# Attention on halves of TensorE's array: scores on 64 rows each, outputs side by side on 64 columns each

## The chip, the core and the metric

The kernel runs on one core of one Trainium2 chip. Its time is the device time of one execution in microseconds (us). Most executions of one kernel agree within 0.3%. TensorE (PE in the profile) multiplies and writes to PSUM, VectorE (DVE) and ScalarE (ACT) read PSUM and compute, GpSimd (POOL) does elementwise work and some DMAs, and SyncE (SP) issues most DMAs. Weight loads of TensorE stand apart as PEld.

## The reference, cut to what matters

Two large blocks follow each other; the change is in the first one's attention. There are 512 tokens, 16 query heads of width 64 in 2 groups of 8, and each group shares one key and one value head:

```
def one_block(args):                       # i: one of 4 blocks of 128 queries
    kb = dynamic_slice(kp, start, 2 * BLOCK); vb = dynamic_slice(vp, start, 2 * BLOCK)
    sc = einsum('bqhgd,bkhd->bhgqk', qi, kb) * ATTN_SCALE
    sc = where(mask, sc, NEG_INF)          # causal, window of 128
    sc = concatenate([sc, sink], axis=-1)
    p = softmax(sc, axis=-1)[..., :-1]
    return einsum('bhgqk,bkhd->bqhgd', p, vb)
```

## The kernel before

Activations lie with features on the 128 partitions and the 512 tokens along the free axis. `kv[:, 0]` holds the keys of both groups: group 0 on partitions 0 to 63, group 1 on partitions 64 to 127. `kv[:, 1]` holds the values. The queries in `q` are permuted so that each of its 8 tiles of 128 partitions holds one head of group 0 (partitions 0 to 63) above one head of group 1 (64 to 127).

`attention` walks through 16 cases: 4 blocks `b` of 128 queries times 4 pairs `hg` of query tiles. `weights(b, hg)` makes the scores of four heads (L325, tile `q` stationary, keys moving), masks them (L328), and takes the softmax on DVE and ACT (L338 to L350). A block sees 256 keys, the first one 128. Before the change a score matmul contracts over all 128 partitions, against `kz`, a copy of the keys in which the other group's 64 partitions are zero; GpSimd makes `kz` (L244, L245) early in the block. `apply(b, hg)`, called one case later, transposes the weights by TensorE (L363), copies them out of PSUM (L365, tile `pT`), and multiplies by the transposed values `vt` (L367): group `r` writes 64 PSUM partitions of `po`, so its matmul uses 64 columns of the array, and both its key blocks run one after the other before the next group's transposes begin. `split` (L84, L85) then writes the result as a high and a low part into `ya`.

These matmuls are f32; each shows in the trace as two MATMUL rows with a weight load each. The other matmuls of this stretch, `mm3` at L111 (gates on `xb`, the pooling's projection on `yp`), are f32r with 512 columns and show as one. They are the work that fills the attention: after each case `block1` issues one more unit out of the list `fill` (three gates, then `mix`, then gates and `pool_up` in turn). A list scheduler of the framework sets the order of the instructions on each engine ahead of time; on the chip each engine takes its instructions in that order and waits on semaphores. `mix` is the pooling branch: DVE and ACT make `pf` (L399 to L401, L84, L85), which the matmuls at L408 read.

Elsewhere in the kernel, matmuls on parts of the array already stand side by side. In the RWKV chunks (second block) L1252 gives two heads 64 columns each, and L1147 and L1159 give two heads 64 rows and 64 columns each:

```
for hh in range(2):                                        # L1252: heads are (hh, z, zb)
    nc.tensor.matmul(py[zb], vt[:, zb], sk[:, hh, 0, 1], start=True, stop=True)
for hh in range(2):                                        # L1147: rows z, columns zb
    nc.tensor.matmul(py[zb], s0[z], C[c][2][z, d], start=True, stop=True)
for hh in range(2):                                        # L1159: rows z, columns z
    nc.tensor.matmul(pq[z], C[c][0][z, d], s0[z], start=True, stop=True)
```

Here `z` is one half of the partitions and `zb` the other. L1104 uses 64 rows and all 128 columns, one head at a time.

Of the kernel before, what the change touches and what calls it, by code (L numbers as in the profile page):

```python
# [8 lines left out]
F32 = mybir.dt.float32  # L9
# [11 lines left out]
P = 128  # L21
T = 512
# [27 lines left out]
class Kern:  # L50
# [154 lines left out]
    def block1(self):  # L205

        nc, tc = self.nc, self.tc
        st = ExitStack()
        p1 = self.c1 = st.enter_context(tc.tile_pool(name="b1", bufs=1))
        wk = st.enter_context(tc.tile_pool(name="b1w", bufs=2))  # L210
# [10 lines left out]
        nc.scalar.copy(rs, self.rstd_row(self.rstd_cols(ss, 1e-5)))  # L221
        self.consts1()
        kv = p1.tile([P, 2, T], F32, name="kv")
        kz = p1.tile([P, 2, T], F32, name="kz")
        q = self.res.tile([P, KD, T], F32, name="q", tag="h")
        pz = p1.tile([P, 4, T], F32, name="pz")
        ya = self.Apool.tile([P, 2, KD, T], F32R, name="ya", tag="A")
        yah, yal = ya[:, 0], ya[:, 1]

        def zout(dst, m):  # L230
            f = AF.Identity if m < 14 else AF.Sigmoid

            def out(_, ps):
                t = self.t()
                nc.vector.tensor_tensor(t, ps, rs, op=OP.mult)
                nc.scalar.activation(dst, t, f, bias=self.v("b_in", m))
            return out

        X = self.rhs(xh, xl)
        for m in range(10):  # L240
            self.dense("w_in", X, zout(kv[:, m] if m < 2 else q[:, m - 2], m), [m])
        for r in range(2):
            z, zz = slice(r * 64, r * 64 + 64), slice(64 - r * 64, 128 - r * 64)
            nc.gpsimd.memset(kz[zz, r], 0.0)  # L244
            nc.gpsimd.tensor_copy(kz[z, r], kv[z, 0])  # L245
        for m in range(10, 14):
            self.dense("w_in", X, zout(pz[:, m - 10], m), [m])
        pf = p1.tile([P, 2, 4, T], F32R, name="pf", tag="t2")
# [21 lines left out]
            fill += [lambda m=m + GA1: gate(m)] * (m < 8 - GA1) + [lambda m=m: pool_up(m)]  # L270
        fill += [lambda m=m: gate_a(m) for m in range(8)]
        steps, done, n = 0, 0, len(fill)
        for _ in self.attention(wk, kv, kz, q, yah, yal):
            steps += 1
            while done < min(n, (steps - 1) * FA):
                fill[done]()
                done += 1
# [26 lines left out]
        st.close()  # L304
        return h, xg, ss

    def attention(self, wk, kv, kz, q, yah, yal):
        nc = self.nc
        vt = wk.tile([P, 4, P], F32, name="vt", bufs=1)
        ps = self.aux().rearrange("p (b c) -> p b c", b=4)  # L310
        for b in range(4):
            nc.tensor.transpose(ps[:, b], kv[:, 1, b * P:(b + 1) * P], self.ident)
        nc.scalar.copy(vt, ps)
        sink = self.sink
        cases = [(b, hg) for b in range(4) for hg in range(4)]
        S = {}

        def weights(b, hg):
            nk = P if b == 0 else 2 * P
            k0 = 0 if b == 0 else (b - 1) * P  # L320
            s = S[b, hg] = wk.tile([P, 2, 2, 2 * P], F32, name="sc", tag="sc", bufs=3)
            pr = [self.aux().rearrange("p (h k) -> p h k", h=2) for _ in range(2)]
            for i in range(2):
                for r in range(2):
                    nc.tensor.matmul(pr[r][:, i, :nk], q[:, hg * 2 + i, b * P:(b + 1) * P],  # L325
                                     kz[:, r, k0:k0 + nk], start=True, stop=True)
            for r in range(2):
                nc.vector.scalar_tensor_tensor(  # L328
                    s[:, r, :, :nk], pr[r][:, :, :nk], 0.125,
                    self.amask[:, None, 2 * P - nk:].to_broadcast([P, 2, nk]),  # L330
                    op0=OP.mult, op1=OP.add)
            mx = wk.tile([P, 2, 2], F32, name="mx", tag="mx")
            ng = wk.tile([P, 2, 2], F32, name="ng", tag="ng")
            sm = wk.tile([P, 2, 2], F32, name="sm", tag="sm")
            es = wk.tile([P, 2, 2], F32, name="es", tag="es")
            rc = wk.tile([P, 2, 2], F32, name="rc", tag="rc")
            sk = sink[:, :, hg * 2:hg * 2 + 2]
            nc.vector.tensor_reduce(mx, s[:, :, :, :nk], axis=AX.X, op=OP.max)  # L338
            nc.vector.tensor_tensor(mx, mx, sk, op=OP.max)
            nc.vector.tensor_scalar(ng, mx, -1.0, None, op0=OP.mult)  # L340
            nc.vector.tensor_tensor(es, sk, mx, op=OP.subtract)
            for r in range(2):
                for i in range(2):
                    nc.scalar.activation(s[:, r, i, :nk], s[:, r, i, :nk], AF.Exp, bias=ng[:, r, i:i + 1],
                                         accum_out=sm[:, r, i:i + 1])
            nc.scalar.activation(es, es, AF.Exp)
            nc.vector.tensor_tensor(sm, sm, es, op=OP.add)
            nc.vector.reciprocal(rc, sm)
            for r in range(2):
                nc.vector.tensor_tensor(s[:, r, :, :nk], s[:, r, :, :nk],  # L350
                                        rc[:, r, :, None].to_broadcast([P, 2, nk]), op=OP.mult)

        def apply(b, hg):
            nk = P if b == 0 else 2 * P
            k0 = 0 if b == 0 else (b - 1) * P
            s = S.pop((b, hg))
            po = self.aux()[:, :2 * P]
            nb = nk // P
            for r in range(2):
                pt = self.aux().rearrange("p (b h q) -> p b h q", b=2, h=2)  # L360
                for kb in range(nb):
                    for i in range(2):
                        nc.tensor.transpose(pt[:, kb, i], s[:, r, i, kb * P:(kb + 1) * P], self.ident)  # L363
                pT = wk.tile([P, 2, 2 * P], F32, name="pT", tag="pT", bufs=3)
                nc.scalar.copy(pT[:, :nb], pt[:, :nb].rearrange("p b h q -> p b (h q)"))  # L365
                for kb in range(nb):
                    nc.tensor.matmul(po[r * 64:r * 64 + 64], vt[:, k0 // P + kb, r * 64:r * 64 + 64], pT[:, kb],  # L367
                                     start=kb == 0, stop=kb == nb - 1)
            self.split(po.rearrange("p (h q) -> p h q", h=2),
                       yah[:, hg * 2:hg * 2 + 2, b * P:(b + 1) * P],  # L370
                       yal[:, hg * 2:hg * 2 + 2, b * P:(b + 1) * P])

        for i, c in enumerate(cases):
            weights(*c)
            if i:
                apply(*cases[i - 1])
            yield 1
        apply(*cases[-1])
        yield 1

# [1320 lines left out]
```

## Time and profile before

| | |
|---|---|
| three timed runs, median | 2801.33 us (2794.91 to 2803.78) |
| the profiled execution | 2801.58 us, of which the span of instructions is 2799.8 us |
| PE busy | 2661.8 us (95%) |
| DVE, ACT, POOL busy | 1929.1 us (69%), 1222.7 us (44%), 746.6 us (27%) |
| the attention, first score matmul to last output matmul | about 97 to 245 us of the span |

Busy time is a share of the whole span; what counts here is who waits for whom within the attention's 148 us. A matmul's own duration in the trace overlaps with the next one's, so the time that it takes from TensorE is read from the start of one row to the start of a later one.

### The profile page before, as it was taken

The numbers are of one execution on the slowest core, as the hardware profiler recorded it, in microseconds if no ns is written. First come the engines' busy times: TensorE is split into PE (matmuls) and PEld (weight loads), VectorE is DVE, ScalarE is ACT, GpSimd is POOL, SyncE is SP. The second block draws the span as 40 slices with busy tenths as digits, with TensorE's granted clock in tenths as the row PEclk, the third lists the DMA queues.
The fourth block names the chain that finished last, engine by engine and source line by source line (L and its number), as shares of the span: only waits on it lengthen the run. The fifth ranks groups of instructions, "written<-read, shape, count | busy, mean of one in ns | idle before, by whom it ended". The sixth has DMA issues, their size and how long they took to land.

```text
span 2799.8 us, 38104 instructions
## 1 busy us (share of the span) xinstructions
PE 2661.8 (95%) x13941; PEld 2202.5 (79%) x13941; DVE 1929.1 (69%) x3742; ACT 1222.7 (44%) x2124; POOL 746.6 (27%) x807
## 2 busy tenths in 40 slices
PE   8999999799999999999999998898899989999997
PEld 6777888789987788888888886676667778888886
DVE  4664579997666778887778858877687765545336
ACT  4664354566532333333333336445555545222234
POOL 0100110000022345454545511443544513111002
PEclk9999999899999999999999998999899999999999
DMA  3112322467798878898899952121000013222332
GB/s 122 61 42 76 118 101 84 141 200 241 245 346 288 300 267 324 327 330 314 321 331 332 323 176 91 61 61 46 1 1 1 1 46 107 91 98 91 98 98 76
DMA packets 173356, 446.15 MB, mean 159 GB/s; under 512 B 14192, under 2 KB 76784, under 8 KB 170992
## 3 DMA queue, kind: packets, MB, share of 16 engines
q1 hardware_dynamic: 136304, 309.47, 32.8%
q0 software_dynamic: 36864, 134.23, 13.3%
q8 instruction: 110, 1.80, 0.3%
q14 instruction: 78, 0.64, 0.1%
HBM read 404.33 MB, written 37.22 MB: 158 GB/s over the span
## 4 chain that ended last, share of the span: by engine, by line
PE 69%; DVE 14%; DMA 5%; POOL 4%; issue 4%; ACT 4%; SPq 0%; DVEq 0%; POOLq 0%; ACTq 0%
PE mm L111 46%; PE aux L782 10%; DMA ga<-gad 3%; PE mm L782 2%; DVE wlo L85 2%; PE aux L607 1%; PE mm L1285 1%; PE aux L367 1%; PE aux L325 1%; POOL gl_E L1379 1%; POOL gr L694 1%; PE aux L1212 1%; DVE gl_K L1388 1%; POOL t L915 1%; DMA wraw<-in_v_dram 1%
## 5 line engine op out<-in xcount | busy, mean ns | idle before, releaser
L84 ACT CAST whi<-wraw 128x1024 fp32r<-128x1024 f32 (+2 forms) x439 | 454.1, 1035 | 920.4 <-PE mm L111 764.2
L85 DVE TENSOR_TENSOR wlo<-wraw,whi 128x1024 fp32r<-128x1024 f32 (+2 forms) x439 | 569.1, 1297 | 319.6 <-ACT whi L84 295.9
L111 PE MATMUL mm<-xb,whi 128*128 128x384 f32 (+1 forms) x2656 | 732.8, 356 | 13.9 <-ACT whi L84 13.3
L111 PEld LDWEIGHTS mm<-xb,whi 128*128 128x128 f32 x2656 | 483.6, 190 | 59.2 <-ACT whi L84 28.5
L111 PE MATMUL mm<-xb,wlo 128*128 128x384 f32 (+1 forms) x1328 | 472.8, 356 | 11.7 <-DVE wlo L85 11.7
L694 POOL DMA_INDIRECT gr<-in_u_dram,gid x128 | 192.2, 1501 | 605.3 <-DVE ga L755 495.3
L111 PEld LDWEIGHTS mm<-xb,wlo 128*128 128x128 f32 x1328 | 252.2, 190 | 40.7 <-DVE wlo L85 21.8
L782 PE MATMUL aux<-wlo,wh 128*128 128x512 f32 x640 | 255.4, 399 | 12.3 <-DVE wlo L85 12.2
L694 POOL DMA_INDIRECT gr<-in_v_dram,gid x128 | 194.2, 1517 | 235.3 <-DVE ga L755 106.3
L782 PE MATMUL aux<-whi,wl 128*128 128x512 f32 x640 | 253.4, 396 | 0.0
L782 PE MATMUL aux<-whi,wh 128*128 128x512 f32 x640 | 253.2, 396 | 0.0
L111 PE MATMUL mm<-fx,whi 128*128 128x512 f32 (+1 forms) x736 | 223.2, 386 | 0.0
L111 PE MATMUL mm<-fp,whi 128*128 128x512 f32 (+1 forms) x732 | 200.6, 360 | 1.1 <-ACT fp L84 0.5
L711 DVE SCALAR_TENSOR_TENSOR yg<-gr,ag,yg 128x1024 f32<-128x1024 f32 x127 | 163.1, 1285 | 4.3 <-DMA gr<-in_v_dram,gid 1.8
L707 DVE SCALAR_TENSOR_TENSOR jk<-gr,xtd 128x1024 bf16<-128x1024 f32 x128 | 156.4, 1222 | 9.5 <-DMA gr<-in_u_dram,gid 7.1
L111 PEld LDWEIGHTS mm<-fx,whi 128*128 128x128 f32 x736 | 135.7, 188 | 30.8
L111 PE MATMUL mm<-x,whi 128*128 128x512 f32 x432 | 148.0, 424 | 8.4 <-DVE h L792 7.5
L782 PEld LDWEIGHTS aux<-wlo,wh 128*128 128x128 f32 x640 | 120.5, 188 | 43.1 <-DVE wlo L85 20.0
L111 PEld LDWEIGHTS mm<-fp,whi 128*128 128x128 f32 x732 | 129.6, 189 | 26.3 <-DVE fp L85 1.7
L111 PE MATMUL mm<-fx,wlo 128*128 128x512 f32 (+1 forms) x368 | 141.8, 385 | 0.0
L782 PEld LDWEIGHTS aux<-whi,wl 128*128 128x128 f32 x640 | 120.6, 188 | 24.6
L782 PEld LDWEIGHTS aux<-whi,wh 128*128 128x128 f32 x640 | 120.7, 189 | 24.4
(491 smaller groups left out, 4703.4 us busy)
## 6 DMA issues: line engine op xcount, KB each, us to landing
wraw<-in_uT_dram SPq DMA_DIRECT2D x128, 512.0 KB
wraw<-in_v_dram SPq DMA_DIRECT2D x128, 512.0 KB
wraw<-in_w_in_dram SPq DMA_DIRECT2D x57, 512.0 KB
Gd<-stg SPq DMA_DIRECT2D x24, 1024.0 KB
gt<-Gd SPq DMA_DIRECT2D x16, 1536.0 KB
wraw<-in_ffn_gate_dram SPq DMA_DIRECT2D x22, 512.0 KB
wraw<-in_ffn_up_dram SPq DMA_DIRECT2D x22, 512.0 KB
wraw<-in_ffn_down_dram SPq DMA_DIRECT2D x17, 512.0 KB
```

What stands on the lines that cost most here:

```text
L84: self.nc.scalar.copy(hi, src)
L85: return (eng or self.nc.vector).tensor_tensor(lo, src, unr(hi), op=OP.subtract)
L111: self.nc.tensor.matmul(ps, a, b, start=first and n == 1, stop=last and n == 3 * kt)
L325: nc.tensor.matmul(pr[r][:, i, :nk], q[:, hg * 2 + i, b * P:(b + 1) * P], kz[:, r, k0:k0 + nk], start=True, stop=True)
L367: nc.tensor.matmul(po[r * 64:r * 64 + 64], vt[:, k0 // P + kb, r * 64:r * 64 + 64], pT[:, kb], start=kb == 0, stop=kb == nb - 1)
L607: nc.tensor.matmul(ps[:, t], j1[:, z, t4 + t], oi[:, t4 + t], start=z == 0, stop=z == 1)
L694: dep(nc.gpsimd.indirect_dma_start(out=r, out_offset=None, in_=(A["u"], A["v"])[z], in_offset=bass.IndirectOffsetOnAxis(ap=gid[:, n:n + 1] ...
L707: i = nc.vector.scalar_tensor_tensor(jk, r, 1.0, xf, op0=OP.mult, op1=OP.mult, accum_out=ag[:, n:n + 1])
L711: i = nc.vector.scalar_tensor_tensor(yg, r, ag[:, n:n + 1], yg, op0=OP.mult, op1=OP.add)
L782: nc.tensor.matmul(acc[f][t], a[:, tk], b[:, fs].rearrange("p k g -> p (k g)"), start=n == 0 and j == 0, stop=n == P - 1 and j == 2)
L915: nc.gpsimd.tensor_tensor(s, z[:, :T], z[:, 2:], op=OP.add)
L1212: nc.tensor.matmul(ps, BK[:, 0, d], AR[:, :, d], start=True, stop=True)
```

## The change

The score matmuls read 64 partitions of `q` and of `kv[:, 0]` directly, group 0 on the array's rows 0 to 63 and group 1 on rows 64 to 127; groups alternate from one matmul to the next. `kz` with its two fills and two copies on GpSimd is gone. In `apply` the transposes and copies of both groups come first, and the output matmuls then alternate between the groups, that is between the two halves of the array's columns. `pT` gets a fourth buffer.

```
--- before.py
+++ after.py
@@ -221,7 +221,6 @@
         nc.scalar.copy(rs, self.rstd_row(self.rstd_cols(ss, 1e-5)))
         self.consts1()
         kv = p1.tile([P, 2, T], F32, name="kv")
-        kz = p1.tile([P, 2, T], F32, name="kz")
         q = self.res.tile([P, KD, T], F32, name="q", tag="h")
         pz = p1.tile([P, 4, T], F32, name="pz")
         ya = self.Apool.tile([P, 2, KD, T], F32R, name="ya", tag="A")
@@ -239,10 +238,6 @@
         X = self.rhs(xh, xl)
         for m in range(10):
             self.dense("w_in", X, zout(kv[:, m] if m < 2 else q[:, m - 2], m), [m])
-        for r in range(2):
-            z, zz = slice(r * 64, r * 64 + 64), slice(64 - r * 64, 128 - r * 64)
-            nc.gpsimd.memset(kz[zz, r], 0.0)
-            nc.gpsimd.tensor_copy(kz[z, r], kv[z, 0])
         for m in range(10, 14):
             self.dense("w_in", X, zout(pz[:, m - 10], m), [m])
         pf = p1.tile([P, 2, 4, T], F32R, name="pf", tag="t2")
@@ -270,7 +265,7 @@
             fill += [lambda m=m + GA1: gate(m)] * (m < 8 - GA1) + [lambda m=m: pool_up(m)]
         fill += [lambda m=m: gate_a(m) for m in range(8)]
         steps, done, n = 0, 0, len(fill)
-        for _ in self.attention(wk, kv, kz, q, yah, yal):
+        for _ in self.attention(wk, kv, q, yah, yal):
             steps += 1
             while done < min(n, (steps - 1) * FA):
                 fill[done]()
@@ -304,7 +299,7 @@
         st.close()
         return h, xg, ss
 
-    def attention(self, wk, kv, kz, q, yah, yal):
+    def attention(self, wk, kv, q, yah, yal):
         nc = self.nc
         vt = wk.tile([P, 4, P], F32, name="vt", bufs=1)
         ps = self.aux().rearrange("p (b c) -> p b c", b=4)
@@ -320,10 +315,12 @@
             k0 = 0 if b == 0 else (b - 1) * P
             s = S[b, hg] = wk.tile([P, 2, 2, 2 * P], F32, name="sc", tag="sc", bufs=3)
             pr = [self.aux().rearrange("p (h k) -> p h k", h=2) for _ in range(2)]
+
             for i in range(2):
                 for r in range(2):
-                    nc.tensor.matmul(pr[r][:, i, :nk], q[:, hg * 2 + i, b * P:(b + 1) * P],
-                                     kz[:, r, k0:k0 + nk], start=True, stop=True)
+                    z = slice(r * 64, r * 64 + 64)
+                    nc.tensor.matmul(pr[r][:, i, :nk], q[z, hg * 2 + i, b * P:(b + 1) * P],
+                                     kv[z, 0, k0:k0 + nk], start=True, stop=True)
             for r in range(2):
                 nc.vector.scalar_tensor_tensor(
                     s[:, r, :, :nk], pr[r][:, :, :nk], 0.125,
@@ -356,15 +353,19 @@
             s = S.pop((b, hg))
             po = self.aux()[:, :2 * P]
             nb = nk // P
+            pTs = []
             for r in range(2):
                 pt = self.aux().rearrange("p (b h q) -> p b h q", b=2, h=2)
                 for kb in range(nb):
                     for i in range(2):
                         nc.tensor.transpose(pt[:, kb, i], s[:, r, i, kb * P:(kb + 1) * P], self.ident)
-                pT = wk.tile([P, 2, 2 * P], F32, name="pT", tag="pT", bufs=3)
+                pT = wk.tile([P, 2, 2 * P], F32, name="pT", tag="pT", bufs=4)
                 nc.scalar.copy(pT[:, :nb], pt[:, :nb].rearrange("p b h q -> p b (h q)"))
-                for kb in range(nb):
-                    nc.tensor.matmul(po[r * 64:r * 64 + 64], vt[:, k0 // P + kb, r * 64:r * 64 + 64], pT[:, kb],
+                pTs.append(pT)
+
+            for kb in range(nb):
+                for r in range(2):
+                    nc.tensor.matmul(po[r * 64:r * 64 + 64], vt[:, k0 // P + kb, r * 64:r * 64 + 64], pTs[r][:, kb],
                                      start=kb == 0, stop=kb == nb - 1)
             self.split(po.rearrange("p (h q) -> p h q", h=2),
                        yah[:, hg * 2:hg * 2 + 2, b * P:(b + 1) * P],
```

The scheduler lays the first block's attention out anew on PE, DVE and ACT; GpSimd loses the four `kz` instructions, SP is as before, and the order behind the attention is as before on every engine. In the listings below one row is one matmul of the program (two rows of the trace where it is f32 and no transpose).

First place, PE just ahead of the pooling's first matmuls (L408, now L409), at 122.16 to 129.84 us of the trace. Before:

```order
L367 MATMUL aux<-pT,vt 64x256
L363 MATMUL aux<-ident,sc 128x128 x2
L325 MATMUL aux<-kz,q 128x256 x3
L367 MATMUL aux<-pT,vt 64x256
L325 MATMUL aux<-kz,q 128x256
L363 MATMUL aux<-ident,sc 128x128 x2
L367 MATMUL aux<-pT,vt 64x256
L363 MATMUL aux<-ident,sc 128x128 x2
L325 MATMUL aux<-kz,q 128x256 x2
L367 MATMUL aux<-pT,vt 64x256
L325 MATMUL aux<-kz,q 128x256 x2
L408 MATMUL mm<-pf,whi 128x512 x2
```

The same place now:

```order
L368 MATMUL aux<-pT,vt 64x256 x2
L322 MATMUL aux<-kv,q 128x256 x4
L361 MATMUL aux<-ident,sc 128x128 x4
L368 MATMUL aux<-pT,vt 64x256 x2
L322 MATMUL aux<-kv,q 128x256 x4
L409 MATMUL mm<-pf,whi 128x512 x2
```

The output matmuls, which stood alone in four places, stand in two pairs, and the score matmuls in two fours; two of the transposes have moved out of this place.

Second place, PE in the first case with 256 keys after `mix` (from about 148 us of the trace). Before:

```order
L325 MATMUL aux<-kz,q 128x256 x4
L363 MATMUL aux<-ident,sc 128x128 x4
L111 MATMUL mm<-yp,whi 128x512 x2
L111 MATMUL mm<-yp,wlo 128x512
L111 MATMUL mm<-yp,whi 128x512 x2
L111 MATMUL mm<-yp,wlo 128x512
L367 MATMUL aux<-pT,vt 64x256 x2
L363 MATMUL aux<-ident,sc 128x128 x4
```

The same place now:

```order
L322 MATMUL aux<-kv,q 128x256 x4
L361 MATMUL aux<-ident,sc 128x128 x8
L111 MATMUL mm<-yp,whi 128x512 x2
L111 MATMUL mm<-yp,wlo 128x512
L111 MATMUL mm<-yp,whi 128x512 x2
L111 MATMUL mm<-yp,wlo 128x512
L111 MATMUL mm<-yp,whi 128x512
L368 MATMUL aux<-pT,vt 64x256
L111 MATMUL mm<-yp,whi 128x512
L368 MATMUL aux<-pT,vt 64x256 x3
```

All eight transposes of a case come first, then its four output matmuls; here the scheduler has put one L111 between the first of the four and the other three.

## Rows read from the trace of the kernel before

**Rows 1.** The page: span, and the chain that ended last by line.

```profile
span 2799.8 us, 38104 instructions
...
PE mm L111 46%; PE aux L782 10%; DMA ga<-gad 3%; PE mm L782 2%; DVE wlo L85 2%; PE aux L607 1%; PE mm L1285 1%; PE aux L367 1%; PE aux L325 1%; POOL gl_E L1379 1%; POOL gr L694 1%; PE aux L1212 1%; DVE gl_K L1388 1%; POOL t L915 1%; DMA wraw<-in_v_dram 1%
```

**Rows 2.** Windows: length; PE, PEld, DVE, ACT, POOL busy (instructions); PEclk; DMA share, GB/s.

```profile
122.16:129.84 7.68, 7.16 (x31) 4.10 (x30) 7.36 (x20) 5.26 (x10) 0.00 (x0) 1.00 0.13 34
129.84:140.33 10.49, 7.73 (x22) 5.39 (x21) 10.14 (x21) 8.96 (x20) 0.00 (x0) 0.67 0.14 50
140.33:245.26 104.93, 104.93 (x481) 73.33 (x480) 67.51 (x146) 67.37 (x165) 0.00 (x0) 1.00 0.16 48
```

**Rows 3.** Waits, 97 to 247 us: who waited for whom; total, times, longest.

```profile
DVE t L235 <- PE mm L111: 11.8, 8, 3.5
...
DVE ya L85 <- ACT ya L84: 10.8, 8, 3.8
DVE sc L328 <- PE aux L325: 10.0, 9, 2.0
...
DVE t L258 <- PE mm L111: 7.2, 5, 3.1
DVE sm L347 <- ACT es L346: 6.9, 5, 2.4
...
PE mm L408 <- ACT pf L84: 2.5, 1, 2.5
```

**Rows 4.** Tile kz: instructions; ns min/median/max, first and last start in us, forms.

```profile
L325 PE MATMUL aux<-kz,q x128: 270/379/483, 97.4 to 230.2; 128*128 128x256 f32 x96, 128*128 128x128 f32 x32
...
L245 POOL COPY kz<-kv x2: 613/992/1370, 31.5 to 32.9; 64x512 f32<-64x512 f32 x2
```

**Rows 5.** Line L367, the output matmuls.

```profile
L367 PE MATMUL aux<-pT,vt x112: 379/379/431, 107.6 to 244.4; 128*64 128x256 f32 x112
```

**Rows 6.** Timeline of PE: start and length in us, line, rows*columns of the array, count.

```profile
153.61 0.40 PE L111 MATMUL mm<-yp,whi 128*128 128x512 f32 x1
153.94 1.08 PE L367 MATMUL aux<-pT,vt 128*64 128x256 f32 x4
154.95 0.50 PE L111 MATMUL mm<-yp,whi 128*128 128x512 f32 x1
155.28 0.39 PE L111 MATMUL mm<-yp,wlo 128*128 128x512 f32 x1
155.52 1.89 PE L325 MATMUL aux<-kz,q 128*128 128x256 f32 x8
157.06 0.82 PE L111 MATMUL mm<-xb,whi 128*128 128x512 f32 x2
157.71 0.39 PE L111 MATMUL mm<-xb,wlo 128*128 128x512 f32 x1
```

**Rows 7.** Timeline of PE in the second block: matmuls on parts of the array.

```profile
1977.49 0.44 PE L1252 MATMUL aux<-rc_sk,rc_vt 128*64 128x128 f32 x4 [0.25 <-POOL rc_sk L1249]
1977.86 0.69 PE L1095 MATMUL aux<-alo,lora 64*128 64x512 f32 x1
...
1983.34 1.12 PE L1104 MATMUL aux<-wlo,lora 64*128 64x512 f32 x2
1984.39 0.33 PE L1232 MATMUL aux<-ident,rkv 128*128 128x128 f32 x1
...
2083.39 0.33 PE L1147 MATMUL aux<-rc_RH,rw_S 64*64 64x128 f32 x2
2083.40 0.33 PE L1159 MATMUL aux<-rw_S,rc_PH 64*64 64x64 f32 x4
...
2092.07 0.65 PE L1147 MATMUL aux<-rc_RH,rw_S 64*64 64x128 f32 x8
2092.65 0.60 PE L1285 MATMUL mm<-rc_Ap,rc_SL 128*128 128x128 f32 x3
```

**Rows 8.** Window after the wait of L408: columns as in Rows 2.

```profile
133.80:138.00 4.20, 4.16 (x11) 3.01 (x12) 3.85 (x10) 3.49 (x7) 0.00 (x0) 0.50 0.36 125
```

More of the change, by code (lines that the diff above doesn't have):

```diff
@@ L223, in block1 @@
         kv = p1.tile([P, 2, T], F32, name="kv")
-        kz = p1.tile([P, 2, T], F32, name="kz")
         q = self.res.tile([P, KD, T], F32, name="q", tag="h")
@@ L241, in block1 @@
             self.dense("w_in", X, zout(kv[:, m] if m < 2 else q[:, m - 2], m), [m])
[L242 to L245, printed above, removed]
         for m in range(10, 14):
@@ L272, in block1 @@
         steps, done, n = 0, 0, len(fill)
-        for _ in self.attention(wk, kv, kz, q, yah, yal):
+        for _ in self.attention(wk, kv, q, yah, yal):
             steps += 1
@@ L305, in block1, with attention @@
         return h, xg, ss
-    def attention(self, wk, kv, kz, q, yah, yal):
+    def attention(self, wk, kv, q, yah, yal):
         nc = self.nc
@@ L324, in weights @@
                 for r in range(2):
-                    nc.tensor.matmul(pr[r][:, i, :nk], q[:, hg * 2 + i, b * P:(b + 1) * P],
-                                     kz[:, r, k0:k0 + nk], start=True, stop=True)
+                    z = slice(r * 64, r * 64 + 64)
+                    nc.tensor.matmul(pr[r][:, i, :nk], q[z, hg * 2 + i, b * P:(b + 1) * P],
+                                     kv[z, 0, k0:k0 + nk], start=True, stop=True)
             for r in range(2):
@@ L358, in apply @@
             nb = nk // P
+            pTs = []
             for r in range(2):
@@ L363, in apply @@
                         nc.tensor.transpose(pt[:, kb, i], s[:, r, i, kb * P:(kb + 1) * P], self.ident)
-                pT = wk.tile([P, 2, 2 * P], F32, name="pT", tag="pT", bufs=3)
+                pT = wk.tile([P, 2, 2 * P], F32, name="pT", tag="pT", bufs=4)
                 nc.scalar.copy(pT[:, :nb], pt[:, :nb].rearrange("p b h q -> p b (h q)"))
-                for kb in range(nb):
-                    nc.tensor.matmul(po[r * 64:r * 64 + 64], vt[:, k0 // P + kb, r * 64:r * 64 + 64], pT[:, kb],
+                pTs.append(pT)
+            for kb in range(nb):
+                for r in range(2):
+                    nc.tensor.matmul(po[r * 64:r * 64 + 64], vt[:, k0 // P + kb, r * 64:r * 64 + 64], pTs[r][:, kb],
                                      start=kb == 0, stop=kb == nb - 1)
```

## The prediction

> **What bounds the kernel now.** I read the page first. Two output lines of attention, L367 and L325, hold 1% each of the chain that ended last, and L111 holds 46% [rows 1]: in the attention TensorE's own work is on the path. The windows say where that holds. From 140.33 to 245.26 us PE is busy without a gap, DVE 67.5 and ACT 67.4 of 104.9 us [rows 2]; there the stretch is as long as PE's list of work. From 122.16 to 140.33 it is otherwise: DVE is busy 7.36 of 7.68 and 10.14 of 10.49 us, and PE is not [rows 2]; L408 waits there 2.5 us in one piece for ACT's `pf` [rows 3]. So a faster PE pays behind 140 us, pays ahead of 122 us, and does not pay between. What follows the attention keeps its order, and its start moves with the attention's end.
>
> **Prices.** All are distances between starts. An L111 takes 0.24 us (155.28 to 155.52). Eight rows of L325 and two L111 take 2.19 us (155.52 to 157.71), so a 256-column f32 row takes (2.19 - 0.48) / 8 = 0.214 us [rows 6]; a 128-column one is taken as half, 0.107, a 512-column one as double. To go from the whole array to 64 columns and back costs extra: 153.61 to 153.94 is 0.33 instead of 0.24; four rows of L367 take 1.01 instead of 0.86; the L111 behind them 0.33 instead of 0.24 [rows 6]. That is 0.33 us a round trip, which I split into 0.14 going in (0.09 of waiting, 0.05 for a first weight load that nothing hides) and 0.19 coming out. For 64 rows the nearest is L1104: two 512-column rows take 1.05 us where 4 x 0.214 = 0.86 is work [rows 7], so the first load of 128 columns costs about 0.09 and going in 0.18.
>
> **Overlap of halves.** The trace shows both halves of the array at work at once. L1252 has the form of the new output matmuls, groups alternating over halves of columns: its four rows take 0.37 us up to the next start (1977.49 to 1977.86). Less 0.05 and 0.10 of switching that is 0.22, two turns of 0.107 and not four. L1147's eight rows on opposite quarters take 0.58 us (2092.07 to 2092.65), less switching 0.43: four turns for eight rows [rows 7]. No row shows two halves of rows with all 128 columns, the new scores' form. Nearest are L1147 and L1159: they start 0.01 us apart, on quarters that share columns and differ in rows [rows 7]. So I take full overlap for both forms; the bound from the other side is none for the scores.
>
> **The sum on PE.** (1) Scores: 96 rows at 0.214 and 32 at 0.107 [rows 4] are 24.0 us; every four keeps its two groups alternating, so they fall to 12.0. Gain 12.0. (2) Outputs: 112 rows [rows 5] at 0.214 are 24.0 us. In the new order six of the twelve cases with 256 keys have all four output matmuls together (2 x 0.428 = 0.86 us); six have one alone and three later, as at the second place, and the three take two turns of 0.428 (1.28 in all). The first block's four cases have three pairs (0.43 each) and two lone ones (0.86). Sum 5.14 + 7.70 + 2.14 = 15.0, gain 9.0. (3) Switches: before, 32 lots of output matmuls make 32 round trips, 10.6 us. Now the order enters 64 columns 23 times and 64 rows 16 times, six of these straight from the one to the other, and comes back to the whole array 33 times: 23 x 0.14 + 16 x 0.18 + 33 x 0.19 = 12.4. Loss 1.8. Together PE's list shrinks by 12.0 + 9.0 - 1.8 = 19.2 us.
>
> **What PE's list doesn't give.** (4) The first place. Before: 16 rows of scores (3.42), 8 of outputs (1.71), four round trips (1.32); now 1.71, 0.86 and six switches (1.02). PE comes to the pooling's matmuls 2.9 us sooner against a DVE that is 96% busy, whose list there is the same work in nearly the same order. So the wait at L409 grows by what was saved: loss 2.9 (bounds 0 and 2.9; DVE's load puts it at the upper end). (5) Behind 140 us. The chain from a case's scores over DVE, ACT and DVE to its transposes doesn't get shorter, and 14 or so of the 105 us of PE's work that covered it go. DVE's 67.5 us still fit. Of DVE's idle time 29.0 us is spent waiting for PE (11.8 + 10.0 + 7.2) and shrinks along with PE; 17.7 us is waiting for ACT (10.8 + 6.9) [rows 3] and doesn't by itself. Bounds: nothing, as PE has no gap now, and some 13 us, if all of that 17.7 falling into the eleven of fifteen cases behind 140 us came out on PE. I take 0.25 us a case, 2.8, near the lower end, because fifteen to twenty L111 stand between scores and transposes in every other case, as before.
>
> (6) `kz`: its copies end by about 34 us and its first reader starts at 97.4 [rows 4]; with 63 us of dense work on PE in between nothing waits for them, so their going is worth nothing. Were that cover gone, the copies would cost at most 1.37 + 0.61 us. The fourth `pT` buffer costs nothing on any engine.
>
> Sum: 19.2 - 2.9 - 2.8 = 13.5 us. The profiled execution took 2801.58 us (2799.8 and 1.8 outside the span), the median run 2801.33. Forecast **2788 us**.
>
> **A rule against it.** L1252's rows show pairs side by side although each f32 matmul of the program is two rows of the trace: if rows started strictly in the program's order, the second row of one half would hold back the first row of the other, and its four rows would need three turns, 0.32 us and not the 0.22 measured; L1147's eight would need five, 0.54 and not 0.43 [rows 7]. The Trainium skill, page "TensorE: Matmul & The Clock Gate", section "Part 3: Packing small matmuls — row/col tiling", states that matmuls start and end strictly in order. By that rule the trace disagrees for these forms. It stays a rival, since the scores' own form is not in the trace.
>
> **The rivals.**
> - *Turns in order* (the rule above). A four needs five turns instead of four, a pair three instead of two: 12 fours of scores and 6 of outputs at 0.214, 3 pairs at 0.214, and 0.3 for the short scores, 4.8 us. Time 2793. For it: nothing measured. Against: [rows 7].
> - *The softmax chain becomes the bound.* The upper bound of (5): 19.2 - 2.9 - 13 = 3.3 gained, 2798. For it: DVE and ACT are at 64% already and share one chain per case [rows 2]. Against: PE has no gap there.
> - *Only the columns overlap.* Halves of rows with all columns are the one form not seen. The 12.0 go; the first place then has 1.7 less to lose, and (5) half: 19.2 - 12.0 - 1.2 - 1.4 = 4.6, 2797.
> - *The change doesn't do what it says*, neither form overlaps: only the switches remain, 1.8 us slower, 2803.
> - *Slower by the clock.* After its 2.5 us wait at L408, PE ran at a granted clock of 0.50, the 1.2 GHz level, for all of 133.8 to 138 us [rows 8]; the same work takes twice as long there. If shorter lists open waits in every case and the clock falls with them, each us of work at that level costs one more. It decides from 13.5 us of work on: there the gain is gone. With half of the 91 us behind 140, the time is 2834. For it: the wait at L408 did it once. Against: the clock is 1.00 over the 104.9 us behind [rows 2].
>
> **How the numbers follow.** Forecast 0.60; turns in order 0.12; softmax chain 0.10; only columns 0.07; neither 0.05; clock 0.06. About 0.3%, 8.4 us, is what a measurement of this kernel can tell from no change: faster means below 2793. The forecast and half of the first rival lie below, 0.66; the rest of it, the chain, the columns and neither lie within, 0.28; the clock, slower, 0.06. The range for 8 in 10: from all 19.2 us but for a little of (4), 2783, up to the chain's 2798, which leaves out the last two rivals and the tails. The forecast's own range, with (4) and (5) between their bounds short of the rivals, is 2783 to 2793.
>
> **What would show it.** Right: from the start of a four of 256-column scores to the row behind it about 0.86 us and switching, where eight rows took 1.71; its second row 0.01 us behind the first; fours of outputs likewise; PE's wait at L409 near 5 us instead of 2.5; the last output matmul near 232 us instead of 244.4. Wrong: score rows 0.21 apart one by one (only columns, or neither); a row 0.107 to 0.214 late at the turn from one half to the other (in order); PE idle ahead of L361 or L368 behind 140 us by a us or more a case (the chain); a granted clock under 1.00 behind 140 us.

## The result and the profile of the changed kernel

The changed kernel takes 2784.7 us (median of 5 runs, 2782.1 to 2785.8) against 2801.3 for the kernel before on the same chip: a ratio of 0.9948, 95% interval 0.9933 to 0.9963. The forecast was 2788.

Lines after the change: scores L322 (was L325), transposes L361 (L363), copies L363 (L365), outputs L368 (L367), the pooling's matmuls L409 (L408). First the page, whose rows answer to [rows 1]:

```profile
span 2784.0 us, 38120 instructions
...
PE mm L111 42%; PE aux L783 7%; POOL gr L695 5%; DMA ga<-gad 3%; DVE wlo L85 2%; PE mm L783 1%; PE aux L608 1%; PE mm L1286 1%; POOL gl_E L1380 1%; PE aux L1213 1%; PE aux L368 1%; DVE gl_K L1389 1%; POOL t L916 1%; DMA wraw<-in_v_dram 1%; 
```

The scores (L325 before, which the prediction counts among the output lines) have left the chain that ended last, the outputs still hold 1%. Then the windows, with the columns of [rows 2]: ahead of the pooling's matmuls, those matmuls and what stands among them, and from there to the last output.

```profile
119.79:126.56 6.77, 4.71 (x28) 2.54 (x29) 6.67 (x20) 4.99 (x10) 0.00 (x0) 1.00 0.00 0
126.56:135.93 9.37, 6.58 (x22) 4.74 (x23) 9.12 (x20) 8.76 (x21) 0.00 (x0) 0.82 0.16 56
135.93:231.28 95.35, 94.30 (x480) 62.22 (x479) 68.84 (x147) 67.20 (x166) 0.00 (x0) 1.00 0.17 52
```

DVE is still busy nearly all the time in the first two, and PE is not; behind them PE now has 1.05 us of gaps and the granted clock is 1.00. Waits from 97 to 232 us, with the columns of [rows 3]:

```profile
DVE t L253 <- PE mm L111: 8.9, 8, 2.4
...
PEld aux L368 <- ACT pT L363: 6.7, 18, 0.7
...
DVE sc L325 <- PE aux L322: 3.5, 7, 1.0
...
PE mm L409 <- ACT pf L84: 3.5, 2, 2.5
...
PE aux L361 <- DVE sc L347: 1.1, 2, 0.6
```

DVE waits less for the scores (3.5 instead of 10.0 us); PE waits more for ACT's `pf` at L409 (3.5 instead of 2.5) and, new, at L361. Now a four of scores in the timeline of PE; the second fence is the same place cut to 143.05 to 143.2 us, so that only the rows then running are counted:

```profile
142.81 0.39 PE L111 MATMUL mm<-xb,wlo 128*128 128x512 f32 x1
143.13 1.13 PE L322 MATMUL aux<-kv,q 64*128 64x256 f32 x8
144.19 1.09 PE L361 MATMUL aux<-ident,sc 128*128 128x128 f32 x8
```

```profile
143.13 0.49 PE L322 MATMUL aux<-kv,q 64*128 64x256 f32 x2
```

Eight rows take 1.06 us to the next start; a row of the first two lasts 0.48 us and both lie within 0.49, so they start 0.01 us apart. That is four turns of 0.21 and 0.2 of switching.

**The ruler for what follows.** All kernels have the same L111 matmuls, so I measure the stretch from the 336th start of L111, ahead of the first score, to the 701st, behind the last output. It is 166.3 us before (96.70 to 263.00) and 153.4 now (95.43 to 248.79): 12.9 us gained. The span outside the stretch lies between 2623.7 and 2639.6 us over the profiles of this study, with the same work, so single times differ by several us that have nothing to do with the change; the 3.7 us between 12.9 and the medians' difference of 16.6 are within that.

One thing besides the order differs from profile to profile: for how long PE ran at a granted clock of 0.50, the 1.2 GHz level, behind its wait at the pooling. Here are these windows for the kernel before, for a second profile of it, and for the changed kernel:

```profile
133.30:140.13 6.83, 6.29 (x17) 4.75 (x18) 6.48 (x12) 5.52 (x10) 0.00 (x0) 0.50 0.22 77
```

```profile
133.95:137.36 3.41, 3.41 (x12) 2.42 (x11) 3.34 (x6) 2.98 (x6) 0.00 (x0) 0.50 0.57 154
```

```profile
131.23:134.65 3.42, 3.42 (x11) 2.81 (x12) 3.17 (x7) 2.83 (x6) 0.00 (x0) 0.50 0.45 153
```

The second profile of before has a stretch of 165.3 us, 1.0 less than the first, and all of that lies ahead of the 421st L111 (48.3 and 47.3 us); from there to the 701st both take 118.0. So at the same time spent at 0.50 the change gains 12.0 us, and 1.0 of the 12.9 goes with the clock of one profile. In every kernel of this study the clock is 1.00 from the 421st L111 to the 701st; ahead of it the last column of the next table says how long it was 0.50.

### The profile page after: what moved, and what is told of

It is laid out like the page before. It is cut to its first block, busy times and chain, and to the rows that moved or that the text cites. A ratio compares the mean times of both kernels' runs of the same rounds, so it can differ in the third digit from the quotient of the medians.

```text
span 2784.0 us, 38120 instructions
## 1 busy us (share of the span) xinstructions
PE 2643.2 (95%) x13941; PEld 2186.3 (79%) x13941; DVE 1928.7 (69%) x3742; ACT 1221.1 (44%) x2124; POOL 745.6 (27%) x803
## 4 chain that ended last, share of the span: by engine, by line
PE 61%; DVE 14%; POOL 8%; issue 8%; DMA 5%; ACT 4%; SPq 0%; DVEq 0%; POOLq 0%; ACTq 0%
PE mm L111 42%; PE aux L783 7%; POOL gr L695 5%; DMA ga<-gad 3%; DVE wlo L85 2%; PE mm L783 1%; PE aux L608 1%; PE mm L1286 1%; POOL gl_E L1380 1%; PE aux L1213 1%; PE aux L368 1%; DVE gl_K L1389 1%; POOL t L916 1%; DMA wraw<-in_v_dram 1%; ACT whi L84 1%
## 5 line engine op out<-in xcount | busy, mean ns | idle before, releaser
L111 PE MATMUL mm<-xb,whi 128*128 128x384 f32 (+1 forms) x2656 | 731.6, 356 | 12.4 <-ACT whi L84 11.5
L111 PEld LDWEIGHTS mm<-xb,whi 128*128 128x128 f32 x2656 | 482.2, 190 | 59.6 <-ACT whi L84 26.9
L111 PE MATMUL mm<-xb,wlo 128*128 128x384 f32 (+1 forms) x1328 | 472.5, 356 | 12.1 <-DVE wlo L85 12.0
L111 PEld LDWEIGHTS mm<-xb,wlo 128*128 128x128 f32 x1328 | 251.8, 190 | 41.4 <-DVE wlo L85 23.3
L783 PE MATMUL aux<-wlo,wh 128*128 128x512 f32 x640 | 255.1, 399 | 13.0 <-DVE wlo L85 12.9
L111 PE MATMUL mm<-fx,whi 128*128 128x512 f32 (+1 forms) x736 | 223.2, 385 | 0.0
L111 PE MATMUL mm<-fp,whi 128*128 128x512 f32 (+1 forms) x732 | 200.7, 360 | 1.0 <-ACT fp L84 0.5
L708 DVE SCALAR_TENSOR_TENSOR jk<-gr,xtd 128x1024 bf16<-128x1024 f32 x128 | 156.4, 1222 | 7.3 <-DMA gr<-in_u_dram,gid 5.0
L111 PEld LDWEIGHTS mm<-fx,whi 128*128 128x128 f32 x736 | 135.7, 188 | 30.9
L111 PE MATMUL mm<-x,whi 128*128 128x512 f32 x432 | 148.2, 424 | 8.4 <-DVE h L793 7.5
L111 PEld LDWEIGHTS mm<-fp,whi 128*128 128x128 f32 x732 | 129.6, 189 | 26.3 <-DVE fp L85 1.6
L111 PE MATMUL mm<-fx,wlo 128*128 128x512 f32 (+1 forms) x368 | 141.8, 385 | 0.0
L84 ACT CAST wh<-ga 128x384 fp32r<-128x384 f32 x128 | 65.6, 513 | 170.2 <-PE mm L783 128.6
```

Source lines behind the costliest of these rows:

```text
L84: self.nc.scalar.copy(hi, src)
L111: self.nc.tensor.matmul(ps, a, b, start=first and n == 1, stop=last and n == 3 * kt)
L708: i = nc.vector.scalar_tensor_tensor(jk, r, 1.0, xf, op0=OP.mult, op1=OP.mult, accum_out=ag[:, n:n + 1])
L783: nc.tensor.matmul(acc[f][t], a[:, tk], b[:, fs].rearrange("p k g -> p (k g)"), start=n == 0 and j == 0, stop=n == P - 1 and j == 2)
```

## The experiments

The kernels were timed in five groups, each beside runs of the kernel before, whose median moved between 2798.3 and 2802.5 us. So kernels of different groups are compared by their ratios, and the intervals reach 3 to 5 us to either side: most neighbours in this table differ by less, and what is said of them rests on the stretch, on one profile each.

| kernel | median us (runs) | ratio to before, 95% | stretch us | of it at clock 0.50 |
|---|---|---|---|---|
| before | 2801.3 (5) | | 166.3 | 6.8 |
| before, a second profile | 2798.4 (1) | | 165.3 | 3.4 |
| the changed kernel | 2784.7 (5) | 0.9948 (0.9933 to 0.9963) | 153.4 | 3.4 |
| scores alone | 2797.8 (12) | 0.9988 (0.9978 to 0.9998) | 161.3 | 3.4 |
| outputs alone | 2789.5 (11) | 0.9964 (0.9952 to 0.9975) | 156.4 | 3.4 |
| scores by group | 2790.1 (7) | 0.9960 (0.9946 to 0.9975) | 156.8 | 3.4 |
| second group first | 2782.2 (6) | 0.9937 (0.9921 to 0.9953) | 149.2 | 6.8 |
| the same, scores against kz | 2786.4 (5) | 0.9952 (0.9938 to 0.9965) | 151.4 | 6.8 |
| pooling early | 2784.1 (5) | 0.9944 (0.9930 to 0.9957) | 155.1 | 10.2 |
| second group first and pooling early | 2783.4 (5) | 0.9940 (0.9926 to 0.9953) | 149.2 | 10.2 |
| two cases ahead | 2783.9 (6) | 0.9932 (0.9919 to 0.9946) | 147.4 | 10.2 |
| the same, scores on the whole array | 2782.8 (6) | 0.9936 (0.9923 to 0.9950) | 150.4 | 3.4 |
| outputs later | 2780.4 (6) | 0.9934 (0.9916 to 0.9952) | 142.9 | 10.2 |
| the same, scores on the whole array | 2779.9 (6) | 0.9930 (0.9917 to 0.9942) | 144.4 | 0 |

**Each half alone.** First the scores of the changed kernel with the outputs of the old one:

```
-            for kb in range(nb):          # behind both groups' copies
-                for r in range(2):
+                for kb in range(nb):      # inside the loop over r, behind each copy
                     nc.tensor.matmul(po[r * 64:r * 64 + 64], vt[...], pT[:, kb], ...)
```

> The scores on 64 rows as in the changed kernel, the outputs in the old order (both key blocks of one group behind that group's copy, then the next group). Theory (the two halves work at once, and PE's list is what the attention takes): eight score rows of 256 columns take about 1.07 us up to the next row, 12 us come off the list, sixteen more changes of tile cost about 3, the rest is lost at the pooling: 7 to 10 us faster than before, 5 to 8 us slower than the changed kernel. Rival (the gain comes from the new order around the outputs, with the copies of both groups ahead of them, and not from halves working at once): within 3 us of before.

It gains 2.7 us by the medians, and in the stretch 5.0 against the first profile of before and 4.1 against the second, which has its time at 0.50. All fall short of the theory; the medians' 2.7 lies within the rival's 3 us, the stretch does not. PE's timeline of one case (here L364 are the outputs, L360 the transposes) shows why:

```profile
162.39 1.13 PE L322 MATMUL aux<-kv,q 64*128 64x256 f32 x6
163.44 1.08 PE L364 MATMUL aux<-pT,vt 128*64 128x256 f32 x4
164.45 0.70 PE L322 MATMUL aux<-kv,q 64*128 64x256 f32 x2
165.08 0.33 PE L360 MATMUL aux<-ident,sc 128*128 128x128 f32 x1
```

Where the old output order stays, the scheduler puts an output pair into the four scores. The score left alone has nothing on the other half: six and two rows take 1.05 and 0.63 us, 1.68 together, hardly less than the 1.71 of eight rows on the whole array. Of the twelve fours with 256 keys five are cut so; three more are cut 4 and 4 with both groups in each part, which costs only another switch (0.63 and 0.63 us instead of 1.06). The rows do run side by side, so the rival's reason is not the one. The new output order is what keeps the scores together. Then the outputs alone, with `kz` and its scores as before:

> The outputs in the new alternating order, the scores against the zero-padded keys on the whole array again, the four GpSimd instructions for them too. Theory: eight score rows take 1.71 us as before, four output matmuls 0.9 to 1.5 us depending on when the second copy of the weights is there; 5 to 8 us faster than before, 8 to 11 us slower than the changed kernel; the gains of this kernel and of the one with the scores alone add up to that of the whole change within 3 us. Rival (the new order is what gains): within 3 us of the changed kernel.

11.0 us by the medians, 9.9 in the stretch (9.0 against the second profile of before): the outputs bring most of the change, more than the theory had: beside the overlap, 32 round trips of 0.33 us became 23, 3.0 us. The two kernels' stretches gain 5.0 and 9.9, together 14.9, where the whole change gains 12.9 (against the second profile 13.0 and 12.0).

**In whose order do rows start?**

```
-            for i in range(2):
-                for r in range(2):
+            for r in range(2):
+                for i in range(2):
                     z = slice(r * 64, r * 64 + 64)
```

> The changed kernel with the four score matmuls of a case by group (group 0 twice, then group 1 twice) instead of alternating; nothing else is written differently, the scheduler may move other work. If each half of the array takes its own rows in its own order, however far apart they stand in the program: eight rows still take about 1.07 us, and the time is within 3 us of the changed kernel. If only matmuls that are neighbours in the program run side by side: the second and the third do, the first and the last are alone, six turns, 1.5 us, and the time is about 6 us above. If rows start strictly in the program's order: seven turns of 0.21, 1.7 us, about 9 us above.

PE's timeline of a four whose matmuls stand as 0, 0, 1, 1 in the program; the second fence is again cut, to 143.71 to 143.72 us:

```profile
143.71 1.14 PE L322 MATMUL aux<-kv,q 64*128 64x256 f32 x8
144.78 0.44 PE L361 MATMUL aux<-ident,sc 128*128 128x128 f32 x2
```

```profile
143.71 0.49 PE L322 MATMUL aux<-kv,q 64*128 64x256 f32 x2
```

1.07 us again, with the first two rows running side by side, though four rows of group 0 stand ahead of the first of group 1. So each half takes its own rows in its own order; starting strictly in the program's order is out, and so are neighbours only. That bears on the rule of the Trainium skill (page "TensorE: Matmul & The Clock Gate", section "Part 3: Packing small matmuls — row/col tiling") that matmuls start and end in the program's order: for f32 matmuls on different halves this trace disagrees. The time was missed, though by little: 3.4 us above the changed kernel by the ratios (5.4 by the medians), 3.5 in the stretch. The scheduler laid it out anew and cut two fours, which costs 1.5 us more than the changed kernel's one, and PE's gaps grew by 1.2 (7.2 in the stretch instead of 6.0). At 159.58 us the cut leaves one group on each side of the outputs:

```profile
159.58 1.13 PE L322 MATMUL aux<-kv,q 64*128 64x256 f32 x4
160.64 1.08 PE L368 MATMUL aux<-pT,vt 128*64 128x256 f32 x6
161.65 1.13 PE L322 MATMUL aux<-kv,q 64*128 64x256 f32 x4
```

Four rows of one half take 1.06 us, as long as eight rows of both.

**The outputs' lone turns.** In the changed kernel six fours of outputs stand together; three look like the first here, one like the second, two lie between:

```profile
162.85 1.56 PE L368 MATMUL aux<-pT,vt 128*64 128x256 f32 x8
164.34 0.72 PE L111 MATMUL mm<-yp,whi 128*128 128x512 f32 x2
...
196.00 1.08 PE L368 MATMUL aux<-pT,vt 128*64 128x256 f32 x8
197.02 0.50 PE L111 MATMUL mm<-yp,wlo 128*128 128x512 f32 x1
```

1.49 against 1.02 us for the same eight rows. The weight loads of L368 wait for ACT's copy `pT` (18 times, 6.7 us, above); I took it that group 1's matmul is the one that waits, for the second copy, while group 0's runs alone. In the first of these fours the second copy ends at 163.28 us: two rows start ahead of that, 0.27 us apart, the next four in two pairs from 163.33 us on, and the last two alone again. The test:

```
             for kb in range(nb):
-                for r in range(2):
+                for r in (1, 0):
```

> The changed kernel with the outputs of group 1 issued first in each pair, so that the first output matmul needs the second copy of the weights and the scheduler places all four behind it. Theory (the outputs gained less than reckoned because the group 1 matmul waited for that copy while the group 0 one ran alone): no lone output matmul is left, all four take about 1.0 us with the switching in each case, the time falls by 2 to 6 us below the changed kernel. Rival (the wait only moves to the first matmul and PE stands still for it): PE idle ahead of the outputs grows by as much, and the time is within 1.5 us of the changed kernel or above it.

```profile
163.58 1.08 PE L368 MATMUL aux<-pT,vt 128*64 128x256 f32 x8
164.60 0.51 PE L111 MATMUL mm<-yp,whi 128*128 128x512 f32 x1
```

All twelve fours now take 1.02 us and the four pairs 0.58. The time is 3.1 us below the changed kernel by the ratios (2.5 by the medians), within their intervals, and 4.1 in the stretch; the rows show the theory, the time agrees with it. Part of it is paid back in waits of PE from 138 to 250 us:

```profile
PE aux L361 <- DVE sc L347: 1.7, 5, 0.4
...
PE aux L368 <- ACT pT L363: 0.4, 2, 0.2
```

**The pooling's place.** The step that makes `pf` on DVE and ACT is issued after the first gate, its matmuls where they were:

```
-        fill = [lambda m=m: gate(m) for m in range(GA1)] + [mix]
+        fill = [lambda: gate(0), mix[0], lambda: gate(1), lambda: gate(2), mix[1]]
```

> The changed kernel with the pooling step cut in two: the elementwise part that makes the pooling's input on DVE and ACT is issued after the first gate, its matmuls on TensorE stay behind the third. Theory (TensorE stands still at the pooling's matmuls, 3.8 us in the changed kernel, because their input is made too late): these waits shrink, the time falls 1.5 to 4 us below the changed kernel. Rival (DVE is the bound of that place, 96% busy before, so the work only changes its order on it): the idle time turns up ahead of the transposes or outputs there, the sum stays within 1.5 us.

> Both at once: outputs of group 1 first in each pair, and the pooling step cut in two. If the two places are independent, the gains of the two single kernels add up: some 4 to 7 us below the changed kernel, about 2778 to 2781 us. If DVE bounds the first place whatever the order: no lower than the kernel with the second group first, about 2782.

PE's waits from 97 to 240 us of the first of the two, and the window of its pooling:

```profile
PE aux L361 <- DVE sc L347: 3.1, 4, 1.9
PE mm L111 <- DVE wlo L85: 2.6, 1, 2.6
PE aux L368 <- ACT pT L363: 1.4, 2, 1.0
```

```profile
104.00:118.60 14.60, 9.15 (x42) 5.80 (x41) 14.01 (x44) 12.49 (x38) 0.95 (x1) 0.76 0.10 27
```

The wait at the pooling's matmuls is gone, but PE's waits are 7.1 us in all, where the rows of the changed kernel add up to 5.5, and DVE is busy 14.01 of 14.60 us. The stretch is 1.8 us longer than the changed kernel's, and with the second group first it is 149.2 either way. The clock works against the early pooling: PE was busy for 9.3 us at 0.50 here and for 3.4 in the changed kernel, which at half the speed is at most 2.9 us; without it the stretch would be at most some 1.2 us below the changed kernel's, still short of the theory's 1.5. By the ratios the two are 1.1 us apart, within their intervals. So the rival holds, by a small margin: DVE sets this place, and what PE waits for there is only a name.

**What are scores on halves worth?** The changed kernel's stretch is 3.0 us shorter than that of the outputs alone, where PE's list has more than twice that (eight rows in 1.06 instead of 1.71 us, twelve times). The same comparison with every four behind the pooling whole:

> Outputs with group 1 first, scores against the zero-padded keys on the whole array as before. Against the kernel with the second group first it tells what the scores on halves are worth when all fours of scores and outputs stay whole. Theory (PE's list): eight rows 1.72 us instead of 1.07, in twelve cases, the short ones 0.25 us each in four, less 0.1 us of switching each: 6 to 8 us slower than that kernel, about 2789. Rival (the softmax chain behind the scores is the bound once the outputs overlap): 4 us slower or less, with more idle time on PE in the kernel with the faster scores.

4.2 us by the medians, 2.1 in the stretch, of it 1.8 behind the 421st L111 (104.5 and 106.3), in the same order on PE and with the same time at 0.50: nearer the rival, whose further sign is there too (gaps of PE behind the 421st L111 of 2.3 us against 0.4). To see whether the softmax chain eats the rest I took it off the path, first by making the weights two cases ahead:

```
-tag="sc", bufs=3)
+tag="sc", bufs=4)
-            if i:
-                apply(*cases[i - 1])
+            if i > 1:
+                apply(*cases[i - 2])
             yield 1
-        apply(*cases[-1])
-        yield 1
+        for c in cases[-2:]:
+            apply(*c)
+            yield 1
```

> The kernel with the second group first, and the weights made two cases ahead of the outputs instead of one, with a fourth buffer for the scores where the zero-padded keys were. Theory (with scores and outputs halved the softmax chain is what PE waits for at the transposes, about 1.7 us at L361 behind a gate's L111 and 2.4 at the first outputs): these waits go, the time falls 2 to 5 us below the kernel with the second group first. Rival (those short waits are only switches of tile, or DVE's load as a whole): within 1 us of it.

> As the kernel two cases ahead, in the same order on every engine, with the scores on all 128 rows of the array against the keys of both groups at once, so each score is the sum of both groups' (this replaces the zero padding and alters the values, not the work). Against that kernel it tells what scores on halves are worth when nothing else moves. Theory (the softmax chain ate the gain): with the chain covered the halves are worth what PE's list says, 5 to 7 us, where it was 2 to 4 with one case ahead. Rival (the switches of tile eat it): 2 to 4 us here too.

Two cases ahead the stretch is 1.8 us shorter than with the second group first, the time by the ratios 1.4, within their intervals. The waits at L361 are gone, and another has come in their place, from 138 to 250 us of the kernel with halves (with whole-array scores it is 0.2):

```profile
PE aux L368 <- ACT pT L363: 2.2, 6, 0.7
```

Scores on halves are worth 3.0 us here in the stretch, 2.8 of it behind the 421st L111 (104.8 and 107.6), and -1.2 by the medians: hardly more than before. So the outputs were moved one case behind their transposes as well (`outputs(*cases[i - 3])` ahead of `apply(*cases[i - 2])`, which then only transposes and copies):

> The kernel two cases ahead, with the outputs of a case issued one case after its transposes, so that a whole case of gates lies between the weights' copies out of PSUM and the matmuls that read them. Theory (in the kernel two cases ahead PE waits for these copies, 2.2 us behind 140 us): those waits go, the stretch from the 336th to the 701st L111 falls from 147.4 to about 144 to 146 us, unless the pooling's place, which is laid out anew, takes some of it. Rival (ACT and DVE as a whole are the bound there): the idle time turns up elsewhere behind 140 us and the stretch stays within 1 us.

> As the kernel with the outputs later, in the same order, with the scores on all 128 rows against the keys of both groups at once (each score is the sum of both groups', the work is that of the scores before). What scores on halves are worth when neither the softmax nor the copies are waited for. Theory (the chain ate half of it): 4.5 to 6.5 us more in the stretch than the kernel with the outputs later, where the pair two cases ahead showed 3.0. Rival (the switches of tile, not the chain): 3 us again.

The stretch of the kernel with the outputs later is 142.9 us, below the theory's 144 to 146, and PE has no wait behind 140 us left. The windows of the two from the 421st start of L111, behind the pooling, to the 701st; halves first:

```profile
139.25:238.66 99.41, 99.23 (x542) 72.92 (x540) 71.11 (x148) 69.93 (x167) 0.00 (x0) 1.00 0.21 67
```

```profile
135.24:240.16 104.92, 104.92 (x542) 80.38 (x540) 71.91 (x149) 71.93 (x167) 0.00 (x0) 1.00 0.21 64
```

PE has next to no gap in either, and the halves save 5.5 us in the nine fours of scores between these two starts, 0.6 each where the rows allow 0.65. Between the same two starts the pair two cases ahead differs by 2.8 us, with ten fours. So the theory holds here, and its whole-stretch number does not: 142.9 and 144.4 are 1.5 apart, and by the medians nothing is left (2780.4 and 2779.9). The other 4.0 us were lost ahead of the 421st L111. The windows from 121 to 134 us of the two:

```profile
121.00:126.00 5.00, 2.28 (x15) 0.99 (x14) 5.00 (x18) 4.96 (x10) 0.00 (x0) 0.84 0.00 0
126.00:130.00 4.00, 4.00 (x13) 2.21 (x13) 4.00 (x7) 2.90 (x6) 0.00 (x0) 0.50 0.00 0
130.00:134.00 4.00, 4.00 (x12) 2.33 (x14) 1.89 (x6) 0.76 (x2) 0.00 (x0) 0.50 0.28 63
```

```profile
121.00:126.00 5.00, 2.88 (x18) 1.97 (x16) 5.00 (x19) 4.94 (x10) 0.00 (x0) 1.00 0.00 0
126.00:130.00 4.00, 4.00 (x21) 2.94 (x19) 4.00 (x7) 3.50 (x8) 0.00 (x0) 1.00 0.00 0
130.00:134.00 4.00, 4.00 (x21) 2.93 (x21) 4.00 (x10) 4.00 (x8) 0.00 (x0) 1.00 0.13 29
```

With halves PE finished its scores sooner and then stood 2.72 us at one place (2.12 with whole scores); behind that its clock was 0.50, the 1.2 GHz level, where the other's was 1.00. The same four rows of outputs, the first behind the wait, take 1.05 and 0.58 us to the next start:

```profile
124.95 1.12 PE L374 MATMUL aux<-pT,vt 128*64 128x256 f32 x4 [2.72 <-ACT pT L362]
126.00 0.48 PE L360 MATMUL aux<-ident,sc 128*128 128x128 f32 x1
```

```profile
125.45 0.65 PE L373 MATMUL aux<-pT,vt 128*64 128x256 f32 x4 [2.12 <-DVE sc L324]
126.03 0.33 PE L359 MATMUL aux<-ident,sc 128*128 128x128 f32 x1
```

From these rows to the next L111 the kernel with halves takes 11.1 us and the other 6.6: that is the 4 us, less the 0.5 by which it left its wait sooner. Whether the shorter scores make the clock fall isn't shown, with one profile of each: two profiles of the kernel before, the same program, differ too (6.8 and 3.4 us at 0.50). The runs of the kernel with halves lie between 2768.4 and 2785.1 us.

**The start.** The profile of before reaches the 336th L111 1.27 us later than that of the changed kernel:

> The kernel before once more, for a second profile: the profile of before reached the first attention score 1.2 us later than all four kernels so far did, also the one that still makes the zero-padded keys. If that is how executions vary at the start and not the work for these keys, this profile starts the attention up to 1.2 us earlier; the length of the attention's stretch, 166.3 us from the 336th to the 701st L111, stays within 0.5 us.

It comes 0.79 us earlier (95.91 instead of 96.70), and the outputs alone, which still make `kz`, 1.14 earlier (95.56): the start varies by itself. The stretch is 0.96 us shorter, more than I allowed, and the clock can account for it: behind the wait at L408 it is 0.61 in 133.06 to 137.20 us, where [rows 8] had 0.50.

## Why the forecast was right, point by point

**Overlap of halves** was right in both forms, with each half's rows in its own order.

**(1) Scores**, forecast 24.0 to 12.0 us. The starts of all 128 rows to the next start sum to 17.1 us; 1.8 of it is waiting behind two fours at the pooling, 3.2 the sixteen times 0.2 us of switching. 12.1 are left, a gain of 11.9.

**(2) Outputs**, forecast 24.0 to 15.0. The starts sum to 21.0; 23 times 0.15 us of switching off, 17.5 are left. Gain 6.5 instead of 9.0: this term was mis-sized. I let a four start when its matmuls stood together; group 0 started ahead, without group 1, because of the copy that was still missing (shown by the kernel with the second group first, where all starts sum to 14.5 with the switching).

**(3) Switches** I can give only as what is left over: PE's busy time in the stretch fell by 15.6 us (162.97 to 147.41); 11.9 and 6.5, less 1.0 of short waits that leave no gap (below), less 15.6 leaves a loss of 1.8, forecast 1.8. Against the second profile of before the busy time fell by 14.6 and 2.8 are left over; that pair has the same time at 0.50, so the meeting of 1.8 with 1.8 is luck.

**(4) The first place**, forecast 2.9: mis-sized too. PE's gaps there grew from 3.3 to 4.8 us, a loss of 1.5, and its last matmul started 4.6 us sooner than before, 3.3 if the start of the stretch is taken off (2.4 against the second profile). The wait at L409 is 3.8 us (3.5 for ACT and 0.3 for DVE) instead of 2.7, and not 5. That DVE bounds the place was right, which pooling early shows; that its list would end at the same time was not.

**(5) The softmax chain**, forecast 2.8. PE's gaps behind the pooling grew from none to 1.05 us, and eight L111 ahead of transposes last 0.36 instead of 0.23 us to the next start, gaps not counted, 1.0: together 2.1 at most, as four of the eight stand at an even 0.32 between two lots of transposes, a place that the order before did not have. The mechanism is shown by the pairs: behind the pooling scores on halves are worth 1.8 us with the chain one case ahead, 2.8 with two, and 5.5 with the copies off the path as well.

**(6)** `kz` worth nothing: nothing in the runs speaks against it.

By these terms PE's list shrank by 16.6 us instead of 19.2 and waits took 3.6 instead of 5.7 (15.6 and 3.6 against the second profile). The two errors point opposite ways, so that the sum of 13.5 met the 12.9 of the stretch, or 12.0 at the same clock, is in part luck; the overlap of halves, which carries most of it, is not. Of the rivals, turns in order, columns only and no overlap are refuted by the rows. The softmax chain took some 2 us and not 13. The slower clock did not come behind the pooling (1.00 from 134.65 us to the end of the attention). At the pooling the changed kernel had it for 3.4 us, and the kernel before for 6.8 and 3.4 in its two profiles, a term that the sum did not have; in the kernel with the outputs later it took 4 us.

The last output started at 230.4 us, forecast near 232.

## What to carry to other kernels

Work on two halves of the array saves time only where both halves have something ready: look at how the scheduler cuts the groups, and let the group whose data come last be issued first. When two units share a chain, halving one's work shows up as a wait at the next link (here transposes, then copies), and the rest of the gain is had only after each link has been given a case of slack. Measure such a change between two fixed points of the program, and compare the granted clock there before the times: two profiles of the kernel before differ by 1.0 us in the stretch, the longer one with twice the time at 0.50. And let timed runs have the last word on what it is worth: by the stretch the kernel with the outputs later is 10.5 us shorter than the changed one, by the ratios 3.9 us faster, and their intervals overlap.

## What the hardware showed that was not expected

Rows on one half start ahead of earlier rows on the other, also where all four rows of one half stand ahead in the program (1.07 us for 0, 0, 1, 1). A group alone on half of the array costs as much as both: four rows 1.06 us, eight rows 1.06. And the granted clock around one wait differs from profile to profile, of the same program too: 6.8 and 3.4 us at 0.50 in two profiles of the kernel before, 0 to 10.2 over all kernels. The same order with shorter scores ran at 0.50 behind a wait of 2.72 us, and with longer ones at 1.00 behind 2.12 us; one profile of each doesn't tell whether the shorter scores are the reason.
